# A hybrid backbone block: the short products of RWKV and of the gated DeltaNet are issued in another order and into other PSUM banks

## The chip, the cores and the metric

The kernel runs on one core of a Trainium2 chip. The metric is the device time of one execution in microseconds (us). Three executions of the kernel before are known; their median counts.

## What is computed

Four layers work on 256 context tokens and 256 latent tokens of width 1024. In each layer a norm with modulation is followed by one wide input projection, three token mixers that each scan the tokens in both directions, a gated sum, an output projection, and a mixture of 16 experts. Two of the mixers matter here, both worked out in chunks of 64 tokens:

- RWKV (8 heads of 64 channels): `S = S * w + (S a) b^T + v k^T`, `y = S r`, for each token in turn.
- GDN, the gated DeltaNet (4 heads of 128 channels), per chunk: `v_new = u - w S`, `o = qg S + A v_new`, `S = S * exp(gl) + kg^T v_new`.

The last layer needs latent tokens only, so its context scans deliver a state and no output.

## The kernel before, in words

All matrix work is fp32. A product in fp32 is two instructions in the trace (a weight load and a matmul each, twice), so counts of instructions are twice the counts of products. The dense projections (line L386) are split into a high and a low part and have one instruction for each product.

**Tokens, heads and halves.** RWKV takes two heads at a time (b = 0 to 3): head p = 0 lies in partitions 0 to 63, head p = 1 in 64 to 127. Each pair has two units (st = 0 context, st = 1 latent), each of four chunks for each direction d. A unit is `rwkv_prep` (decays and scaled keys), then `rwkv_unit`: the 64x64 systems M1, a triangular inverse, and a scan over four steps s. GDN takes one head at a time through `gdn_head`, with a scan of eight steps; its two directions are at chunks of opposite parity, so direction 0 and direction 1 are in opposite halves of the partitions.

A product whose operands lie in 64 partitions uses 64 rows of the array; one whose output has 64 partitions uses 64 columns. The trace writes rows*columns: `64*128` is half of the rows with all columns, `128*64` all rows and half of the columns, `64*64` a quarter.

**The products that the change touches** (z.mm issues one product, `mm(out, weights, moving)`):

- `rwkv_prep`, L814 and L815: for each direction two products of 64 rows by 128 columns over 256 tokens, both into one bank `pw`. In the trace: `ai<-thw,ups` and `ai<-adm,ups`. Two tanh on ScalarE (L818, L819) empty the bank.
- `rwkv_unit`, L888: for each direction and head half four products (64*128) into one bank, then one multiply on VectorE (L889). In the trace: `ai<-AR,BK`.
- `rwkv_unit`, the scan (from L921): each step makes four products of the state, `ac<-X,AR`, into bank `pu`, adds on VectorE (L931), four products with the inverse `ac<-R,Y`, two copies (L937, L938), four products `ac<-UV,BKt` (128*64) that make the next state, and the outputs: for each direction and half one product `ai<-AR,X` (64*64) and one `ai<-M,UV` (128*64) that adds to it, one behind the other, into bank `py` (L954, L955). VectorE then adds up the state (L967), copies or adds `py` to the output tile (L960, L962) and scales the state (L968); the next step's first products need that scaled state.
- `gdn_head`, the scan: each step multiplies the state of each direction with the keys and, where outputs are wanted, with the queries (`bi<-Sg,KQ`, 128*64, L1116 and L1118), makes `R` on VectorE (L1126), two products with the inverse (`bi<-R,Y`), scales on VectorE (L1133, L1135), then for each direction makes the update `bi<-v2g,Kt` (64*128, L1141) in the bank `pv` and adds it to the state on VectorE (L1146). The outputs' last products `bi<-v,Dq` go to bank `pb`.

**Banks.** RWKV's streams have two banks with the tag `ai` and one with `ac`; GDN's has two with the tag `bi`. `psm` takes the next bank of the first tag, `psc` of the second. A bank is given out again when everything that reads it is done.

**What sets the order.** The code runs through a scheduler that puts each engine's instructions in one fixed order. Every product has a due time: a stream starts at a time (`due`), and every product moves it on by its estimated length times the stream's pace (`spend`). Dense projection blocks have due times of their own and stand between the short products; so do the modulation's weights (`ada`, four products of 32 columns side by side for each row block, L305). What is ready and due first goes first. Each engine then runs its list in that order and waits on semaphores.

Of the kernel before, what the change touches and what calls it, by code (L numbers as in the profile page):

```python
# [152 lines left out]
def tile_backbone(ctx: ExitStack, tc: tile.TileContext, A, out, dbg=None, depth=DEPTH):  # L153
# [104 lines left out]
    X = {}  # L258
# [527 lines left out]
    def rwkv_prep(z, b, st, P, R, pr, noy):  # L786
# [17 lines left out]
        tk = slice(t0, t0 + 256)  # L804
# [4 lines left out]
        def c4(t):  # L809
            return t.rearrange("p (c w) -> p c w", c=4)  # L810
        for d in range(2):
            ds_ = slice(64 * d, 64 * d + 64)
            pw = z.psm()
            z.mm(pw[:, 0:256], ups[ds_, 0, :], thw[ds_, tk], start=True, stop=True)  # L814
            z.mm(pw[:, 256:512], ups[ds_, 1, :], adm[ds_, tk], start=True, stop=True)  # L815
# [52 lines left out]
    def rwkv_unit(z, b, st, vb, Y, S, noy, prep, between):  # L868
# [13 lines left out]
        for d in range(2):  # L882
            for p in range(2):
                hp = slice(64 * p, 64 * p + 64)
                ps = z.psm()
                for s in range(4):
                    c = ch(d, s)
                    z.mm(ps[:, s * 128:s * 128 + w_], BK[hp, d, c, :, :], AR[hp, d, c, 0:w_ // 64, :], start=True, stop=True)  # L888
# [33 lines left out]
        for s in range(4):  # L922
            pu = z.psc()
            rhs = Fv[:, :, s, :]
            if X is not None:
                for d in range(2):
                    for p in range(2):
                        hp = slice(64 * p, 64 * p + 64)
                        z.mm(pu[hp, d * 64:d * 64 + 64], AR[hp, d, ch(d, s), 0, :], X[hp, d, :], start=True, stop=True)
                rhs = z.mt([2, 64], "R", 2)  # L930
# [13 lines left out]
            if not noy:  # L944
                py = z.psm()
                lo_first = s < 2
                for d in range(2):
                    q = d * 4 + s
                    sl = d if lo_first else 1 - d
                    for p in range(2):  # L950
                        hp = slice(64 * p, 64 * p + 64)
                        po = py[hp, sl * 64:sl * 64 + 64]
                        if X is not None:
                            z.mm(po, X[hp, d, :], AR[hp, d, ch(d, s), 1, :], start=True, stop=False)  # L954
                        z.mm(po, UV[:, d, s, p, :], M1[:, p, d, s, 64:128], start=X is None, stop=True)  # L955
# [61 lines left out]
    def gdn_head(z, l, h, P, inputs, G, out_, oc, t):  # L1017
# [89 lines left out]
        for s in range(8):  # L1107
            wanted = s * 64 >= oc
            pv = z.psc()
            for d in range(2):  # L1110
                c = order[d][s]
                t, p = c // 2, c % 2
                hp = slice(64 * p, 64 * p + 64)
                first = Sg[d] is None
                if not first:
                    z.mm(pv[hp, 0:128], KQ[:, 0, c, :], Sg[d], start=True, stop=True)  # L1116
                    if wanted:
# [591 lines left out]
```

## Time and profile before

| what | value |
|---|---|
| median of three runs | 5302.02 us (5295.01 to 5309.08) |
| the profiled execution's own time | 5309.78 us |
| its span, first to last instruction | 5308.0 us |
| TensorE (PE) busy | 4849.0 us, 91% |
| VectorE (DVE) busy | 3129.9 us, 59% |
| ScalarE busy | 1440.6 us, 27% |
| GpSimd (POOL) busy | 1405.5 us, 26% |

Busy time of an engine is the time in which at least one of its instructions was under way. A matmul's end is modelled, so the time that a run of products really takes from the engine is read from starts: from its first start to the start of what follows it. Digits of the granted clock are tenths of full speed.

### The profile page before, as it was taken

To read this page: it belongs to the slowest core of one execution; us is meant where nothing else is said; L and a number is where in the kernel's file an instruction comes from. 1 tells how busy PE (TensorE), PEld (TensorE's weight loads), DVE (VectorE), ACT (ScalarE), POOL (GpSimd) and SP (SyncE) were. 2 spreads that over 40 slices of the span, in tenths; PEclk is the share of its full clock that TensorE was granted. 3 is DMA by queue.
4 is the path that set the end of the run, shared out by engine and by line. 5 is a ranking of instruction groups with operands and counts; after the bars stand their busy time and mean duration, and the time that the engine had idled before them with its cause. 6 is when DMAs were issued, how large, how long until landed. Compare 5 with 4: busy or idle time off the path is not lost. (4 is left out here: it accounts for less than half of the span.)

```text
span 5308.0 us, 85225 instructions
## 1 busy us (share of the span) xinstructions
PE 4849.0 (91%) x31882; PEld 3102.1 (58%) x31882; DVE 3129.9 (59%) x8787; ACT 1440.6 (27%) x2796; POOL 1405.5 (26%) x1847
## 2 busy tenths in 40 slices
PE   7999999999999999999998999999998898987798
PEld 4666666653466666666336666666633666666533
DVE  4776656633476766564347676666433677767322
ACT  3332222220233322222014222322311333322211
POOL 3332312320233222233014222222400433323400
PEclk8999999999999999999999999999999899897899
DMA  5333345579632233446983223344698222323598
GB/s 185 101 103 113 119 125 160 188 270 393 248 91 63 67 99 93 149 147 240 387 310 99 65 63 93 100 137 129 207 385 313 74 73 68 86 61 109 188 361 320
DMA packets 677006, 873.59 MB, mean 165 GB/s; under 512 B 336976, under 2 KB 359504, under 8 KB 663792
## 3 DMA queue, kind: packets, MB, share of 16 engines
q1 hardware_dynamic: 676592, 868.14, 48.5%
q8 instruction: 251, 4.11, 0.3%
q14 instruction: 163, 1.34, 0.1%
HBM read 788.47 MB, written 79.51 MB: 164 GB/s over the span
## 5 line engine op out<-in xcount | busy, mean ns | idle before, releaser
L364 POOL TENSOR_TENSOR wlo<-wraw,whi 128x512 fp32r<-128x512 f32 x696 | 942.4, 1359 | 2311.9 <-ACT whi L363 1798.6
L386 PE MATMUL df<-big,whi 128*128 128x512 f32 (+1 forms) x2944 | 982.5, 404 | 80.0 <-DVE mg L479 19.2
L386 PE MATMUL dm<-big,whi 128*128 128x512 f32 (+1 forms) x2368 | 820.0, 415 | 52.5 <-ACT cv L693 31.3
L363 ACT CAST whi<-wraw 128x512 fp32r<-128x512 f32 x696 | 426.0, 617 | 1261.5 <-PE df L386 530.7
L386 PEld LDWEIGHTS df<-big,whi 128*128 128x128 f32 x2944 | 538.4, 198 | 239.6 <-issue 51.2
L386 PE MATMUL df<-big,wlo 128*128 128x512 f32 (+1 forms) x1536 | 605.5, 394 | 22.6 <-POOL wlo L364 22.5
L386 PEld LDWEIGHTS dm<-big,whi 128*128 128x128 f32 x2368 | 447.4, 200 | 184.3 <-issue 45.0
L386 PE MATMUL dm<-big,wlo 128*128 128x512 f32 (+1 forms) x1248 | 508.0, 407 | 8.1 <-POOL wlo L364 8.1
L386 PEld LDWEIGHTS df<-big,wlo 128*128 128x128 f32 x1536 | 304.3, 198 | 86.9 <-POOL wlo L364 27.7
L1595 PE MATMUL df<-mw,big 128*64 128x512 f32 x1024 | 301.2, 610 | 0.0
L386 PEld LDWEIGHTS dm<-big,wlo 128*128 128x128 f32 x1248 | 248.3, 199 | 70.0 <-issue 16.8
L1642 DVE SCALAR_TENSOR_TENSOR big<-bi,der,big 128x256 f32<-128x256 f32 x448 | 191.9, 478 | 118.0 <-PE bi L1639 117.6
L1595 PE MATMUL dm<-mw,big 128*64 128x512 f32 x1024 | 255.5, 594 | 2.1 <-DMA mw<-in_w_dram 1.9
L984 DVE SCALAR_TENSOR_TENSOR cv<-cv,par,cv 128x189 f32<-128x189 f32 (+3 forms) x472 | 230.3, 496 | 13.0 <-ACT cv L981 10.1
L1602 POOL MEMSET mada<- 128x512 f32 x32 | 16.8, 525 | 802.7 <-PE bi L1639 350.7
L414 DVE TENSOR_TENSOR Y<-Y,sv 64x44 f32<-64x44 f32 (+6 forms) x672 | 190.2, 285 | 5.7
L413 DVE TENSOR_TENSOR sv<-Y 64x14 f32<-64x14 f32 (+6 forms) x672 | 188.7, 282 | 6.0
L1595 PEld LDWEIGHTS dm<-mw,big 128*64 128x64 f32 x1024 | 80.7, 137 | 152.4 <-issue 137.9
L697 DVE SCALAR_TENSOR_TENSOR big<-cv,muc,big 128x252 f32<-128x252 f32 (+2 forms) x280 | 140.6, 518 | 17.2 <-ACT big L694 15.5
L1633 DVE SCALAR_TENSOR_TENSOR mlof<-ac,aff,mhif 128x512 fp32r<-128x512 f32 x32 | 24.0, 750 | 212.4 <-ACT mhif L1632 212.4
L210 PE MATMUL ai<-AR,BK 64*128 64x128 f32 (+1 forms) x1024 | 144.1, 303 | 4.5 <-DVE t L775 2.8
L1629 PE MATMUL ac<-mw,mrawf 128*64 128x512 f32 x512 | 139.5, 600 | 8.6 <-ACT mrawf L1623 8.5
(511 smaller groups left out, 8334.0 us busy)
## 6 DMA issues: line engine op xcount, KB each, us to landing
mw<-in_w_dram SPq DMA_DIRECT2D x768, 512.0 KB, 10.3
wraw<-in_w_in_dram SPq DMA_DIRECT2D x536, 256.0 KB, 2.7
adaw<-in_ada_w_dram SPq DMA_DIRECT2D x96, 1024.0 KB, 5.8
gates<-gt SPq DMA_DIRECT2D x114, 256.0 KB, 2.9
wraw<-in_w_branch_dram SPq DMA_DIRECT2D x96, 256.0 KB, 3.0
TU<-zoai SPq DMA_DIRECT2D x128, 128.0 KB, 3.1
wraw<-in_w_out_dram SPq DMA_DIRECT2D x64, 256.0 KB, 5.3
t<-gates SPq DMA_DIRECT2D x61, 256.0 KB, 4.1
```

What stands on the lines that cost most here:

```text
L210: mm(o, a, b, **kw)
L363: se.copy(dst_hi, src)
L364: eng.tensor_tensor(dst_lo, src, dst_hi.bitcast(F32), ALU.subtract)
L386: mm(ps[:, c0:c1], a[:, k % 4, :], bk[:, c0:c1], start=(n == 0), stop=(n == 3 * nk - 1))
L413: ve.tensor_tensor(tv, Xb[:, j + 1:, j:j + 1].to_broadcast(sh), Xb[:, j:j + 1, 0:j].to_broadcast(sh), ALU.mult)
L414: ve.tensor_tensor(Xb[:, j + 1:, 0:j], Xb[:, j + 1:, 0:j], tv, ALU.add)
L697: ve.scalar_tensor_tensor(dst, src, muc[:, 1 + q, rb:rb + 1], dst, ALU.mult, ALU.add)
L984: ve.scalar_tensor_tensor(dst, src, cw[:, cb, t:t + 1], dst, ALU.mult, ALU.add)
L1595: mm(ps[64 * q:64 * q + 64, :], xe[k // 4][:, k % 4, e0 + q, :], wt[q][:, k2 * 512:(k2 + 1) * 512], start=(k == 0), stop=(k == 7))
L1629: mm(py[hf][64 * q:64 * q + 64, :], hT[:, kk, 64 * q:64 * q + 64], wt[q][:, hf * 512:(hf + 1) * 512], start=(kk == 0), stop=(kk == 3))
L1633: ve.scalar_tensor_tensor(yl[hf], py[hf], aff, yh[hf].bitcast(F32), ALU.mult, ALU.subtract)
L1642: ve.scalar_tensor_tensor(xT[:, db, cs_], pcb[:, cs_], der[:, 3, db, s:s + 1], xT[:, db, cs_], ALU.mult, ALU.add)
```

## The change

It reorders products and moves some to other banks; no product, copy or transfer is added or taken away.

- `rwkv_prep`: both directions' banks are taken first; the two `thw` products of the two directions are issued one behind the other, then the two `adm` products.
- `rwkv_unit`, M1: for each direction both head halves' banks are taken, and the products alternate between the halves; the two multiplies on VectorE follow behind all eight.
- The scan: bank `py` is taken at the step's start, the four `AR,X` products stand right behind the four `X,AR` products, and the four `M,UV` products stand together behind the four `UV,BKt` products. Only the first direction's product clears the bank.
- `gdn_head`: `pv` and `pb` are both taken at the step's start; the state's products go keys first for both directions, then queries; the second direction's update goes into `pb`; the two updates are issued together, and the two additions on VectorE follow.

```diff
--- before.py
+++ after.py
@@ -808,11 +808,14 @@
 
         def c4(t):
             return t.rearrange("p (c w) -> p c w", c=4)
+
+        pws = [z.psm() for d in range(2)]
+        for q, src in enumerate((thw, adm)):
+            for d in range(2):
+                ds_ = slice(64 * d, 64 * d + 64)
+                z.mm(pws[d][:, 256 * q:256 * q + 256], ups[ds_, q, :], src[ds_, tk], start=True, stop=True)
         for d in range(2):
-            ds_ = slice(64 * d, 64 * d + 64)
-            pw = z.psm()
-            z.mm(pw[:, 0:256], ups[ds_, 0, :], thw[ds_, tk], start=True, stop=True)
-            z.mm(pw[:, 256:512], ups[ds_, 1, :], adm[ds_, tk], start=True, stop=True)
+            pw = pws[d]
             sg = z.mt([256], "t1", 6)
             tha = z.mt([256], "t1", 6)
             se.activation(sg, pw[:, 0:256], AF.Tanh, scale=0.5, bias=hb[:, 0, d * 4 + b:d * 4 + b + 1])
@@ -880,12 +883,13 @@
         M1 = z.mt([2, 2, 4, 128], "M1")
         w_ = 64 if noy else 128
         for d in range(2):
-            for p in range(2):
-                hp = slice(64 * p, 64 * p + 64)
-                ps = z.psm()
-                for s in range(4):
+            pss = [z.psm() for p in range(2)]
+            for s in range(4):
+                for p in range(2):
+                    hp = slice(64 * p, 64 * p + 64)
                     c = ch(d, s)
-                    z.mm(ps[:, s * 128:s * 128 + w_], BK[hp, d, c, :, :], AR[hp, d, c, 0:w_ // 64, :], start=True, stop=True)
+                    z.mm(pss[p][:, s * 128:s * 128 + w_], BK[hp, d, c, :, :], AR[hp, d, c, 0:w_ // 64, :], start=True, stop=True)
+            for p, ps in enumerate(pss):
                 ve.tensor_tensor(M1[:, p, d, :, 0:w_], ps.rearrange("q (s w) -> q s w", s=4)[:, :, 0:w_],
                                  C[f"m1_{d}"][:, None, 0:w_].to_broadcast([128, 4, w_]), ALU.mult)
 
@@ -927,6 +931,22 @@
                     for p in range(2):
                         hp = slice(64 * p, 64 * p + 64)
                         z.mm(pu[hp, d * 64:d * 64 + 64], AR[hp, d, ch(d, s), 0, :], X[hp, d, :], start=True, stop=True)
+
+
+            lo_first = s < 2
+            po = None
+            if not noy:
+                py = z.psm()
+
+                def po(d, hp):
+                    sl = d if lo_first else 1 - d
+                    return py[hp, sl * 64:sl * 64 + 64]
+                if X is not None:
+                    for d in range(2):
+                        for p in range(2):
+                            hp = slice(64 * p, 64 * p + 64)
+                            z.mm(po(d, hp), X[hp, d, :], AR[hp, d, ch(d, s), 1, :], start=d == 0, stop=False, skip_group_check=True)
+            if X is not None:
                 rhs = z.mt([2, 64], "R", 2)
                 ve.tensor_tensor(rhs, pu[:, 0:128].rearrange("p (d w) -> p d w", d=2), Fv[:, :, s, :], ALU.add)
             for d in range(2):
@@ -942,17 +962,10 @@
                     hp = slice(64 * p, 64 * p + 64)
                     z.mm(pu[hp, 128 + d * 64:192 + d * 64], BKt[:, q, 64 * p:64 * p + 64], UV[:, d, s, p, :], start=True, stop=True)
             if not noy:
-                py = z.psm()
-                lo_first = s < 2
                 for d in range(2):
-                    q = d * 4 + s
-                    sl = d if lo_first else 1 - d
                     for p in range(2):
                         hp = slice(64 * p, 64 * p + 64)
-                        po = py[hp, sl * 64:sl * 64 + 64]
-                        if X is not None:
-                            z.mm(po, X[hp, d, :], AR[hp, d, ch(d, s), 1, :], start=True, stop=False)
-                        z.mm(po, UV[:, d, s, p, :], M1[:, p, d, s, 64:128], start=X is None, stop=True)
+                        z.mm(po(d, hp), UV[:, d, s, p, :], M1[:, p, d, s, 64:128], start=X is None and d == 0, stop=True, skip_group_check=True)
                 a, e = min(s, 3 - s), max(s, 3 - s)
                 yv = c4(Y[:, tk])[:, a::(e - a), :][:, 0:2, :]
                 pyv = py[:, 0:128].rearrange("p (d w) -> p d w", d=2)
@@ -1106,16 +1119,14 @@
         Sg = [None, None]
         for s in range(8):
             wanted = s * 64 >= oc
-            pv = z.psc()
-            for d in range(2):
-                c = order[d][s]
-                t, p = c // 2, c % 2
-                hp = slice(64 * p, 64 * p + 64)
-                first = Sg[d] is None
-                if not first:
-                    z.mm(pv[hp, 0:128], KQ[:, 0, c, :], Sg[d], start=True, stop=True)
-                    if wanted:
-                        z.mm(pv[hp, 128:256], KQ[:, 1, c, :], Sg[d], start=True, stop=True)
+            pv, pb = z.psc(), z.psm()
+            first = Sg[0] is None
+
+            for q in range(0 if first else 2 if wanted else 1):
+                for d in range(2):
+                    c = order[d][s]
+                    hp = slice(64 * (c % 2), 64 * (c % 2) + 64)
+                    z.mm(pv[hp, 128 * q:128 * q + 128], KQ[:, q, c, :], Sg[d], start=True, stop=True)
 
             R = None
             if not first:
@@ -1137,17 +1148,18 @@
                 c = order[d][s]
                 t, p = c // 2, c % 2
                 hp = slice(64 * p, 64 * p + 64)
-                pS = pv[:, 256 + 128 * d:384 + 128 * d]
-                z.mm(pS, Kt[hp, t, :], v2_[hp, :], start=True, stop=True)
+                z.mm((pv, pb)[d][:, 256:384], Kt[hp, t, :], v2_[hp, :], start=True, stop=True)
+            for d in range(2):
+                c = order[d][s]
+                t, p = c // 2, c % 2
+                pS = (pv, pb)[d][:, 256:384]
                 Sn = z.mt([128], "Sg", 4)
                 if Sg[d] is None:
                     ve.tensor_copy(Sn, pS)
                 else:
                     ve.scalar_tensor_tensor(Sn, Sg[d], eL[:, p, t, d, h:h + 1], pS, ALU.mult, ALU.add)
-                first = Sg[d] is None
                 Sg[d] = Sn
             if wanted:
-                pb = z.psm()
                 for d in range(2):
                     c = order[d][s]
                     t, p = c // 2, c % 2
```

## Rows read from the trace of the kernel before

**Rows 1.** The page, parts 1 and 2: TensorE's busy time and granted clock in 40 slices.
```profile
PE 4849.0 (91%) x31882; PEld 3102.1 (58%) x31882; DVE 3129.9 (59%) x8787; ACT 1440.6 (27%) x2796; POOL 1405.5 (26%) x1847
...
PEclk8999999999999999999999999999999899897899
```

**Rows 2.** Busy time by stretch, all engines: the mixers of layers 1 and 3.
```profile
1498.00:2310.00 812.00, 762.82 (x5947) 530.34 (x5948) 553.47 (x1690) 234.67 (x477) 221.11 (x341) 0.97 0.32 96
...
4189.00:4935.00 746.00, 653.67 (x5608) 506.67 (x5608) 544.75 (x1651) 225.78 (x487) 250.15 (x364) 0.90 0.29 80
```

**Rows 3.** Groups by line on PE: xinstructions | busy us, mean ns | idle before, releasers.
```profile
L210 PE MATMUL ai<-AR,BK 64*128 64x128 f32 (+1 forms) x1024 | 144.1, 303 | 4.5 <-DVE t L775 2.8 <-DVE M L889 1.6
L210 PE MATMUL bi<-Sg,KQ 128*64 128x128 f32 x848 | 139.9, 287 | 0.8 <-DVE Sg L1146 0.5 <-ACT ob L1160 0.3
L210 PE MATMUL ai<-M,UV 128*64 128x64 f32 x896 | 138.0, 241 | 1.0 <-DVE UV L937 0.9
L210 PE MATMUL ai<-AR,X 64*64 64x64 f32 x800 | 126.2, 238 | 1.4 <-DVE Y L440 1.2
L210 PE MATMUL bi<-v2g,Kt 64*128 64x128 f32 x512 | 123.5, 321 | 11.6 <-DVE v L1135 6.9 <-DVE Sg L1146 3.0 <-DVE v2g L1133 1.2
...
L210 PE MATMUL ai<-thw,ups 64*128 64x256 f32 x128 | 44.9, 432 | 5.2 <-DVE Y L414 2.2 <-ACT t L819 2.0 <-DVE sv L413 0.9
...
L210 PE MATMUL ai<-adm,ups 64*128 64x256 f32 x128 | 38.8, 386 | 0.0
```

**Rows 4.** Timeline of PE in an RWKV scan: start us, us, engine line op.
```profile
2025.30 0.45 PE L210 MATMUL ac<-UV,BKt 128*64 128x64 f32 x8
2025.58 0.40 PE L210 MATMUL ai<-M,UV 128*64 128x64 f32 x6
2025.91 0.50 PE L386 MATMUL df<-big,wlo 128*128 128x512 f32 x1
...
2029.82 0.32 PE L210 MATMUL ai<-AR,X 64*64 64x64 f32 x2
...
2031.36 0.73 PE L386 MATMUL df<-big,whi 128*128 128x512 f32 x2
...
2032.25 0.45 PE L210 MATMUL ac<-X,AR 64*64 64x64 f32 x8
2032.53 0.28 PE L210 MATMUL ai<-AR,X 64*64 64x64 f32 x2
```

**Rows 5.** Timeline of VectorE in the same step of the scan.
```profile
2031.46 0.29 DVE L960 COPY big<-ai 128x128 f32<-128x128 f32 x1 [1.23 <-PE ai L210]
2031.67 0.28 DVE L968 TENSOR_TENSOR X<-X,scl 128x128 f32<-128x128 f32 x1
```

**Rows 6.** Two stretches of 0.44 us within one run of AR,BK, by tile BK.
```profile
133.02:133.46 0.44, 0.44 (x4) 0.44 (x5) 0.00 (x0) 0.00 (x0) 1.00 0.00 0
133.50:133.94 0.44, 0.44 (x10) 0.44 (x9) 0.00 (x0) 0.00 (x0) 1.00 0.00 0
```

**Rows 7.** Timeline of PE in a GDN scan.
```profile
2060.32 0.48 PE L210 MATMUL bi<-v2g,Kt 64*128 64x128 f32 x2
2060.73 0.43 PE L210 MATMUL bi<-v,Dq 64*64 64x128 f32 x4
...
2061.96 0.65 PE L210 MATMUL bi<-Sg,KQ 128*64 128x128 f32 x4
2062.54 1.12 PE L210 MATMUL ai<-t,cst 128*128 128x512 f32 x2
...
2070.61 0.66 PE L210 MATMUL bi<-Sg,KQ 128*64 128x128 f32 x8
2071.21 0.72 PE L386 MATMUL df<-big,whi 128*128 128x512 f32 x2
```

**Rows 8.** Groups by line and form on VectorE and ScalarE: what empties RWKV's banks.
```profile
L889 DVE TENSOR_TENSOR M<-ai,cst 128x512 f32<-128x512 f32 x112 | 76.7, 688 | 83.4 <-PE ai L210 82.8
...
L818 ACT ACTIVATE t<-ai,hb 128x256 f32<-128x256 f32 x64 | 30.0, 469 | 9.2 <-PE ai L210 8.9
```

## Prediction

> **What bounds the kernel now.** I read the page first. TensorE (PE) is busy 91% of the span, and its granted clock is full speed in all but a few slices [rows 1]. Busy time by stretch then places it: in the three mixers' stretch of layer 1 PE is busy 762.82 of 812 us, VectorE 553.47, at a granted clock of 0.97; in layer 3, whose fillers are half as wide, 653.67 of 746 at 0.90 [rows 2]. So PE sets the pace in the mixers of layers 0 to 2, where all the touched products lie, and a little less in layer 3. The groups by line give the size of what is touched: M1's `AR,BK` 144.1 us, the GDN state products `Sg,KQ` 139.9, the outputs `M,UV` 138.0 and `AR,X` 126.2, the GDN updates `v2g,Kt` 123.5, the prep's two groups 44.9 and 38.8 [rows 3]. That is 755 us of busy time, and hardly any of it is waiting.
>
> Busy time alone doesn't say what a reorder can save; the timeline does. Within one run of `AR,BK` the array goes through a stretch of 0.44 us with 4 instructions while one half of the rows is used, and through an equal stretch with 10 when the second half's products, in the other bank, have come up behind the first's [rows 6]. So two row halves run at once when they write different banks, and the engine starts the second half a little ahead of its turn. Eight instructions of `Sg,KQ` that stand together, both directions, take from 2070.61 to 2071.21, 0.60 us; four of one direction alone take 0.58 [rows 7]. So column halves pair as well. The cost of the old order is that partners seldom stand side by side.
>
> **The change part by part.** Every saving below is PE time, read from starts.
>
> *The scan's outputs.* Three alternating pairs of `AR,X` and `M,UV` take from 2029.82 to 2031.36, 1.54 us, 0.26 for each product [rows 4]. The trace has both shapes in good company: four `X,AR` products take 2032.25 to 2032.53, 0.28 us, and four `UV,BKt` products 2025.30 to 2025.58, also 0.28, which is 0.07 for each product; there, in a unit's first step, where no `AR,X` exists, the `M,UV` products already follow directly [rows 4]. After the change three products of each kind join such runs: 6 x 0.07 = 0.42 us. The saving is 1.54 - 0.42 = 1.1 us a step. There are 800 / 8 = 100 such steps [rows 3], so 112 us. Bounds: 80, if the outputs' runs stand alone and pay for another change of tile shape (about 0.3 us a step), and 130, with the step's first `AR,X` counted too. I take 112, since the code issues them directly behind their like.
>
> [...] The four `X,AR` products use opposite quarters of the array, write one bank, and still need only 0.07 us each [rows 4], and `AR,X` has that very shape. [...]
>
> *M1.* One half streams an instruction in 0.44 / 4 = 0.11 us [rows 6]. For one direction eight products, 16 instructions, paired throughout need 8 x 0.11 plus about 0.2 at the ends, 1.1 us; 64 directions (32 units) make 70 us against 144.1 now [rows 3], a saving of 74 at most. At least it is nothing: the old order already overlaps where two sets meet, and the second direction now waits for the two banks one after the other, as the two multiplies (688 ns each [rows 8]) release them, so its first half may run ahead alone. I take 45, three fifths.
>
> *Prep.* 44.9 + 38.8 = 83.7 us [rows 3]; perfect pairs save 42, none 0. Both products are ready together, but both banks must be free and another stream's product may slip between. I take 25.
>
> *GDN's state products.* A step with outputs pays 2 x 0.58 now and 0.60 when all four stand together [rows 7]: 0.56 saved in 100 of the steps (848 instructions are 84 steps with eight in the first three layers, 16 in the last, and 12 with four [rows 3]), 56 at most. The second direction's state is ready one addition after the first's, so the first may be issued alone as before: at least 0. I take half, 28.
>
> *GDN's updates.* Each takes 2060.32 to 2060.73, 0.41 us [rows 7], and 512 / 4 = 128 steps have two [rows 3]. Their inputs come from one scaling, and they no longer wait for the other's addition in a shared bank. Paired, the two cost about one: 52 saved. Unpaired in one run they still save one change of shape, about 0.2, 26 us. I take 45.
>
> *Banks and waits.* `pb` is now taken at a step's start; it was emptied a scaling, two products and an addition before its first writer, so this costs nothing, and without that cover the wait would be a copy of 0.3 us. `py` is held from the first product of a step instead of the last ones; the next prep is done before the scan starts, so nobody wants it. No DMA moves, and no instruction on the queues of SP and POOL.
>
> The sum is 112 + 45 + 25 + 28 + 45 = 255 us of PE time. How much of it comes off the end? In layers 0 to 2 PE is 94% busy and dense blocks fill what is freed, so I count 0.85; in layer 3 (88% busy, lower clock) 0.6. At a fifth of the sum in layer 3: 204 x 0.85 + 51 x 0.6 = 204 us. The RWKV chain doesn't stand against it: the output copy at 2031.46 waits 1.23 us for the outputs' products, and the scaling of the state at 2031.67 stands queued behind it on VectorE, though its own input had long been ready [rows 5]. The next step's first products wait for that scaling, so those 1.1 us a step are on the chain too. Late next are the dependent steps themselves: VectorE's short operations and the inverse's round trip.
>
> The profiled execution took 5309.78 us, 7.8 above the median of the runs. 5309.8 - 204 = 5106, and beside the median **5098 us**.
>
> **The rivals.** *The chain sets the mixers' length.* For it: each unit's M1, inverse and scan depend on one another, and PE's 6% idle time in layer 1 stays small only as long as fillers last. Against it: PE is busy nearly throughout [rows 2]. Then only what lies on the chain counts, the outputs' 112 us: about 5190.
>
> *Row halves don't pair.* Then M1 and prep give nothing and the updates 26. The three `AR,X` products of a step, six instructions at the 0.11 us of an unpaired half [rows 6], cost 0.66 instead of 0.21, so the outputs lose 45 of their 112: 67 + 28 + 26 = 121, of which 0.8 is 97, so 5205. [...] [Rows 6] speak against the rest, but show 128 columns in one place only.
>
> *The pairs are torn apart.* The scheduler puts dense blocks or the other stream between partners and the saved shape changes come back elsewhere: within 0.3% of 5302. Against it: `X,AR` stands in eights.
>
> *Slower: both of RWKV's banks are closed at once.* M1's and prep's products now fill both banks together, so nothing of RWKV can use one while VectorE or ScalarE empties the other. Price: for each unit two multiplies of 0.69 us that used to run beside products, and four tanh of 0.47 [rows 8], 1.4 + 1.9 = 3.3 us, times 32 units 105 us: 5407. It decides only if RWKV's chain sets the length and the saved 1.1 us a step are lost to another wait.
>
> **How the numbers follow.** A difference under 0.3% (16 us) can't be told from none. Chances: the forecast 0.62, the chain 0.22, no pairing of rows 0.06, torn pairs 0.04, slower 0.06. Faster is the sum of the first three, 0.90. The lower end takes all upper bounds, 130 + 74 + 42 + 56 + 52 = 354, at 0.85 to 0.9: about 310 us, 4990. The upper end takes the chain and the unpaired rows with some room, 5240; the other two cases, 0.10, and some of the tails are left out.
>
> **What would show it.** Right: the groups `AR,X` and `M,UV` fall from 126 and 138 us to about half or less, with runs of eight behind `X,AR` and `UV,BKt`; `v2g,Kt` stands in fours; VectorE's copy of `py` no longer waits over a microsecond before the scaling; PE's busy time in the mixers falls by some 200 us at much the same share. Chain: PE's share in the mixers drops to about 85% and the stretches shrink by under 30 us each. Unpaired rows: `v2g,Kt` in fours of about 0.6 us. Closed banks: long waits of `AR,BK` or `thw,ups` for VectorE and ScalarE, and units further apart. The forecast is wrong if the short groups shrink and the mixers don't.

## The result, and the profile after

The changed kernel takes 5150.62 us (median of four runs, 5146.26 to 5153.63) beside 5305.55 for the kernel before on the same chip (four runs, 5295.01 to 5318.0). The ratio is 0.9706, 95% interval 0.9683 to 0.973: 155 us or 2.9% faster. The forecast was 5098, its range 4990 to 5240. The profiled execution took 5153.63 us with a span of 5151.7, 156.3 us less than before.

The page of the kernel after, parts 1 and 2, TensorE's busy time and granted clock, beside [rows 1]:

```profile
PE 4671.7 (91%) x31882; PEld 2965.9 (58%) x31882; DVE 3135.1 (61%) x8787; ACT 1437.8 (28%) x2796; POOL 1401.7 (27%) x1847
...
PEclk8999999999999999999999999999999899987899
```

The number of instructions is the same and TensorE's busy time is 177 us lower, at the same share of the span. So the gain fits TensorE time that is no longer needed, 0.88 of which came off the end; the experiments below take the parts apart. Busy time by stretch of the kernel after (span of the stretch, then each engine's busy time and count, granted clock, DMA), the mixers of layers 1 and 3, beside [rows 2]:

```profile
1458.00:2217.00 759.00, 711.25 (x5956) 489.95 (x5957) 556.06 (x1691) 234.39 (x479) 220.43 (x342) 0.96 0.34 103
4050.00:4777.00 727.00, 625.29 (x5606) 486.07 (x5605) 542.08 (x1648) 225.65 (x487) 250.19 (x364) 0.89 0.30 82
```

Layer 1's stretch is 53 us shorter for 51.5 us less of TensorE; layer 3's 19 for 28. TensorE's share is 94% as before and 86% (88 before): freed time in layer 1 turns into length in full, in layer 3 by two thirds.

The groups by line on PE (instructions, then busy us and mean ns of one, then idle before them and releasers), beside [rows 3]:

```profile
L210 PE MATMUL ai<-AR,BK 64*128 64x128 f32 (+1 forms) x1024 | 133.4, 308 | 10.4 <-DVE M L893 6.1 <-DVE t L775 1.8 <-POOL BK L867 1.5
...
L210 PE MATMUL bi<-Sg,KQ 128*64 128x128 f32 x848 | 87.7, 287 | 4.4 <-ACT ob L1172 2.2 <-DVE Sg L1160 1.9
L210 PE MATMUL bi<-v2g,Kt 64*128 64x128 f32 x512 | 87.4, 324 | 9.1 <-DVE v2g L1144 8.8 <-DVE v L1146 0.3
...
L210 PE MATMUL ai<-M,UV 128*64 128x64 f32 x896 | 82.6, 229 | 1.9 <-DVE UV L957 1.5
...
L210 PE MATMUL ai<-thw,ups 64*128 64x256 f32 x128 | 45.0, 433 | 3.4 <-DVE sv L413 3.4
...
L210 PE MATMUL ai<-AR,X 64*64 64x64 f32 x800 | 44.4, 221 | 1.6 <-DVE Y L440 1.6
...
L210 PE MATMUL ai<-adm,ups 64*128 64x256 f32 x128 | 39.5, 389 | 0.0
```

Four groups fell far; `AR,BK` fell by 11, the prep's two not at all. Busy time counts pairs that run at once only once, and ends are modelled, so I also summed, for every instruction of a group, the time from its start to the next instruction's start without idle time. These sums, in us, are what the rest of the text calls TensorE time:

| group | before | after | saved | forecast |
|---|---|---|---|---|
| scan: `AR,X`, `M,UV` with `X,AR`, `UV,BKt` beside them | 276.1 | 168.6 | 107.5 | 112 |
| M1: `AR,BK` | 132.2 | 123.2 | 9.0 | 45 |
| prep: `thw`, `adm` | 69.0 | 70.1 | -1.1 | 25 |
| GDN state products: `Sg,KQ` | 122.3 | 75.1 | 47.2 | 28 |
| GDN updates: `v2g,Kt` | 104.3 | 74.2 | 30.1 | 45 |
| dense projections, L386 | 2131 | 2156 | -25 | 0 |
| all of TensorE | 4849 | 4672 | 177 | 255 |

**The scan.** PE's timeline of the kernel after (start, us, operation, tiles, shape, count), one step, beside [rows 4]:

```profile
1952.09 0.33 PE L210 MATMUL ai<-M,UV 128*64 128x64 f32 x2
...
1952.78 0.45 PE L210 MATMUL ac<-UV,BKt 128*64 128x64 f32 x8
1953.06 0.40 PE L210 MATMUL ai<-M,UV 128*64 128x64 f32 x6
1953.40 0.50 PE L386 MATMUL df<-big,whi 128*128 128x512 f32 x1
...
1954.75 0.45 PE L210 MATMUL ac<-X,AR 64*64 64x64 f32 x8
1955.03 0.40 PE L210 MATMUL ai<-AR,X 64*64 64x64 f32 x8
```

From 1953.06 to 1953.40 three outputs pass in 0.34 us behind their like; before, one product of the alternating run cost 0.26. The eight `AR,X` instructions do the same behind `X,AR`. VectorE's timeline of that step, beside [rows 5]; a bracket would show a wait:

```profile
1953.46 0.29 DVE L980 TENSOR_TENSOR X<-ac,X 128x128 f32<-128x128 f32 x1
...
1953.78 0.28 DVE L973 COPY big<-ai 128x128 f32<-128x128 f32 x1
...
1954.09 0.28 DVE L981 TENSOR_TENSOR X<-X,scl 128x128 f32<-128x128 f32 x1
```

The output copy (L973) no longer waits 1.23 us in front of the scaling (L981).

**GDN.** PE's timeline of the kernel after, beside [rows 7]:

```profile
1979.00 0.49 PE L210 MATMUL bi<-v2g,Kt 64*128 64x128 f32 x4
1979.42 0.50 PE L386 MATMUL df<-big,whi 128*128 128x512 f32 x1
...
1986.67 0.66 PE L210 MATMUL bi<-Sg,KQ 128*64 128x128 f32 x8
1987.26 0.50 PE L386 MATMUL df<-big,whi 128*128 128x512 f32 x1
...
1990.40 0.49 PE L210 MATMUL bi<-v2g,Kt 64*128 64x128 f32 x2 [0.45 <-DVE v2g L1144]
1990.81 0.50 PE L386 MATMUL dm<-big,whi 128*128 128x512 f32 x1
1991.24 0.48 PE L210 MATMUL bi<-v2g,Kt 64*128 64x128 f32 x2
```

Eight `Sg,KQ` take 0.59 us, and 74 such eights stand in the trace, 5 before. Four `v2g,Kt` together take 0.42 us, two alone 0.41; in 80 of the 128 steps the two directions stand together.

**M1 and prep.** PE's timeline of the kernel after, an M1 and a prep:

```profile
133.87 1.16 PE L210 MATMUL ai<-AR,BK 64*128 64x128 f32 x16
...
135.87 1.31 PE L210 MATMUL ai<-AR,BK 64*128 64x128 f32 x10
...
138.23 0.71 PE L210 MATMUL ai<-AR,BK 64*128 64x128 f32 x6
...
1981.82 0.70 PE L210 MATMUL ai<-thw,ups 64*128 64x256 f32 x2
1982.35 0.59 PE L210 MATMUL ai<-adm,ups 64*128 64x256 f32 x2
1982.87 0.43 PE L210 MATMUL bi<-R,Y 64*64 64x128 f32 x4
1983.24 0.70 PE L210 MATMUL ai<-thw,ups 64*128 64x256 f32 x2
1983.78 0.59 PE L210 MATMUL ai<-adm,ups 64*128 64x256 f32 x2
```

Here M1's first direction runs as one sixteen, paired, in about 1.1 us (14 runs in the trace have sixteen instructions); the second is torn in ten and six, 2.4 us apart. The prep still issues one direction's two products and then the other's. The fixed order that the scheduler wrote says the same of every unit: in prep it is `thw`, `adm`, `thw`, `adm` in all 32, as before; M1's halves alternate fully in 22 of 32 units for direction 0 and in 6 for direction 1.

### The profile page after: what moved, and what is told of

Same layout as the page of the kernel before. It is cut to its first block, busy times and chain, and to the rows that moved or that the text cites. A ratio compares the mean times of both kernels' runs of the same rounds, so it can differ in the third digit from the quotient of the medians.

```text
span 5151.7 us, 85291 instructions
## 1 busy us (share of the span) xinstructions
PE 4671.7 (91%) x31882; PEld 2965.9 (58%) x31882; DVE 3135.1 (61%) x8787; ACT 1437.8 (28%) x2796; POOL 1401.7 (27%) x1847
## 5 line engine op out<-in xcount | busy, mean ns | idle before, releaser
L386 PE MATMUL df<-big,whi 128*128 128x512 f32 (+1 forms) x2944 | 1001.9, 408 | 87.6 <-ACT gt L546 19.7
L386 PE MATMUL dm<-big,whi 128*128 128x512 f32 (+1 forms) x2368 | 821.2, 415 | 44.6 <-ACT cv L693 31.7
L386 PEld LDWEIGHTS df<-big,whi 128*128 128x128 f32 x2944 | 545.8, 200 | 253.9 <-issue 46.9
L386 PE MATMUL df<-big,wlo 128*128 128x512 f32 (+1 forms) x1536 | 612.0, 398 | 16.6 <-POOL wlo L364 16.6
L386 PEld LDWEIGHTS dm<-big,whi 128*128 128x128 f32 x2368 | 443.0, 199 | 174.6 <-issue 40.5
L386 PE MATMUL dm<-big,wlo 128*128 128x512 f32 (+1 forms) x1248 | 505.6, 405 | 18.3 <-POOL wlo L364 18.3
L386 PEld LDWEIGHTS df<-big,wlo 128*128 128x128 f32 x1536 | 306.3, 199 | 83.8 <-POOL wlo L364 20.9
L386 PEld LDWEIGHTS dm<-big,wlo 128*128 128x128 f32 x1248 | 248.1, 199 | 81.2 <-POOL wlo L364 22.7
L414 DVE TENSOR_TENSOR Y<-Y,sv 64x14 f32<-64x14 f32 (+6 forms) x672 | 193.6, 290 | 5.6
L210 PE MATMUL ai<-AR,BK 64*128 64x128 f32 (+1 forms) x1024 | 133.4, 308 | 10.4 <-DVE M L893 6.1
```

Of the source, the lines that this page charges most:

```text
L210: mm(o, a, b, **kw)
L386: mm(ps[:, c0:c1], a[:, k % 4, :], bk[:, c0:c1], start=(n == 0), stop=(n == 3 * nk - 1))
L414: ve.tensor_tensor(Xb[:, j + 1:, 0:j], Xb[:, j + 1:, 0:j], tv, ALU.add)
```

## The experiments

My theory after the result: the mixers pay for TensorE time, the saving is the scan's and GDN's, and the forecast fell short of 255 because the pairs of M1 and prep were torn by their banks. The main rivals: RWKV's dependent chain is what was shortened; and saved TensorE time is worth less than it seems. Each measured ratio is to the kernel before, run on the same chip beside it.

### The parts alone

The scan's part of the change alone, on the kernel before:

```diff
+            if not noy:
+                py = z.psm()
...
+                            z.mm(po(d, hp), X[hp, d, :], AR[hp, d, ch(d, s), 1, :], start=d == 0, stop=False, skip_group_check=True)
...
-                            z.mm(po, X[hp, d, :], AR[hp, d, ch(d, s), 1, :], start=True, stop=False)
```

> Only the RWKV scan's outputs are moved. Theory (PE time is the bound, and about 0.88 of what a part frees on PE comes off the end: the whole change freed 177 us by starts and gave 156): AR,X, M,UV and the runs they join free about 112 us, so about 5206 us against 5305. Rival (RWKV's chain is the bound): this part is the only one on the chain, so it gives nearly all of the change's 155 us, about 5155.

Measured: 5224.24 us against 5304.21, ratio 0.9848 (0.9832 to 0.9865), 80 us. The four groups fell from 276.1 to 167.8, all of TensorE by 83. That is nearer to the theory than to the rival, but a step of the scan got shorter too: from one `UV,BKt` run to the next of its unit it takes 5.49 us, 6.37 before (medians of 96). This run alone doesn't separate TensorE's time from the chain.

GDN's part alone:

```diff
+            pv, pb = z.psc(), z.psm()
...
+            for q in range(0 if first else 2 if wanted else 1):
+                for d in range(2):
...
+                z.mm((pv, pb)[d][:, 256:384], Kt[hp, t, :], v2_[hp, :], start=True, stop=True)
```

> Only GDN's two edits. Theory (PE time): Sg,KQ and v2g,Kt free about 75 us, so about 5239 us. Rival (RWKV's chain): GDN's stream is not on it, so within 10 us of 5305.

Measured: 5263.18 us, ratio 0.9923 (0.9908 to 0.9938), 41 us. `Sg,KQ` fell to 75.1 and `v2g,Kt` to 78.9; all of TensorE by 51, short of the 75 that the theory had. RWKV's stream, whose dependent steps this edit leaves alone, got shorter by as much: from its first prep to its last `UV,BKt` of a layer it takes 3222 us in the sum of the four layers, 3265 before, and TensorE's idle time stayed (436 and 438). So the gain reached RWKV through TensorE.

Prep and M1 alone:

```diff
+        pws = [z.psm() for d in range(2)]
...
+            pss = [z.psm() for p in range(2)]
+            for s in range(4):
+                for p in range(2):
```

> Only the order of prep's and M1's products. Theory (the pairs don't form, since the two banks come free one after the other and whichever product has its bank goes alone): thw,ups and adm,ups stay at about 75 us by starts, AR,BK falls by about 9; the time is 5290 to 5305, within what can be told. Rival (the order works, and the other parts hid it in the whole change): AR,BK and the prep fall by 40 us or more and the time to about 5265.

Measured: 5311.61 us, ratio 1.0015 (0.9998 to 1.0032): nothing. `AR,BK` fell to 118.2, prep stayed at 69.1, and the dense products grew from 2131 to 2154, so all of TensorE rose by 13.

The change without prep and M1 (both other parts together):

```diff
-        pws = [z.psm() for d in range(2)]
...
-            pss = [z.psm() for p in range(2)]
```

> The change without prep's and M1's part. Theory (these two parts did nothing): 5150 to 5165 us, within 15 us of the whole change. Rival (they gave their forecast 70 us of PE time): about 5210.

Measured: 5172.81 us, ratio 0.9747 (0.9726 to 0.9768), 131 us, above the 5150 to 5165 of the theory. The two parts alone gave 80 and 41, 121 in sum. The whole change is 22 us better (the intervals of the two ratios still touch), with `AR,BK` at 123.2 instead of 141.6 and `v2g,Kt` at 74.2 instead of 84.9. So prep and M1 are worth nothing alone and a little beside the rest; the rise of the dense products (2152 here, 2156 in the whole change) is there with or without them.

### GDN: the order of the state products, or the banks of the updates?

Only the order of the state products, on the kernel before:

```diff
+            for q in range(0 if first else 2 if wanted else 1):
+                for d in range(2):
...
-                    z.mm(pv[hp, 0:128], KQ[:, 0, c, :], Sg[d], start=True, stop=True)
```

> The kernel before with only the order of GDN's state products changed: keys of both directions, then queries of both; the updates stay in one bank, one behind the other's addition. Theory (the pairs come from the two states being ready together, not from the order in the code): Sg,KQ stays above 110 us by starts, the time is 5290 to 5325. Rival (the order makes the pairs): Sg,KQ falls to about 75 us and the time to about 5265.

Measured: 5316.37 us against 5305.89, ratio 1.0021 (1.0004 to 1.0037). The order alone gives no time. `Sg,KQ` did fall to 105.3, below the 110 of the theory: in 91 steps the first direction's product with the keys goes alone and the other three follow together. But all of TensorE rose by 13, with dense products that cost 25 us more. VectorE's timeline of this kernel, the two additions of a step:

```profile
2067.81 0.35 DVE L1143 SCALAR_TENSOR_TENSOR Sg<-Sg,eg,bi 128x128 f32<-128x128 f32 x1 [1.10 <-PE ai L210]
2068.98 0.35 DVE L1143 SCALAR_TENSOR_TENSOR Sg<-Sg,eg,bi 128x128 f32<-128x128 f32 x1 [0.82 <-PE bi L210]
```

The second direction's state is ready 1.17 us after the first's (1.46 in the median of all steps), since its update shares a bank with the first addition; in most steps the first direction's product has been issued by then.

Only the updates in two banks, with the additions behind both, in the old order of the state products:

```diff
-                pS = pv[:, 256 + 128 * d:384 + 128 * d]
-                z.mm(pS, Kt[hp, t, :], v2_[hp, :], start=True, stop=True)
+                z.mm((pv, pb)[d][:, 256:384], Kt[hp, t, :], v2_[hp, :], start=True, stop=True)
```

> The kernel before with only GDN's updates in two banks, both issued ahead of the two additions; the state products keep the old order, two of one direction, then two of the other. Theory (both states come ready together, and the engine starts the second direction's products ahead of its turn where they stand directly behind): Sg,KQ falls to about 75 to 85 us and v2g,Kt to about 80 by starts, as in gdn_only, so 5255 to 5275 us. Rival (the order is needed as well): Sg,KQ stays near 120 us and the time near 5290.

Measured: 5263.71 us, ratio 0.9925 (0.9905 to 0.9944): all of what GDN's part gives. `Sg,KQ` fell to 80.0 here too, `v2g,Kt` to 84.2. VectorE's two additions of a step and then PE's timeline of this kernel:

```profile
2067.30 0.61 DVE L1147 SCALAR_TENSOR_TENSOR Sg<-Sg,eg,bi 128x128 f32<-128x128 f32 x2
```

```profile
2069.62 0.67 PE L210 MATMUL bi<-Sg,KQ 128*64 128x128 f32 x8
2070.22 0.50 PE L386 MATMUL dm<-big,whi 128*128 128x512 f32 x1
```

The two additions now follow each other 0.26 us apart in the median (1.44 in the kernel before), so both states are ready together and both directions' four stand together; and though two products of one direction stand ahead of the other's, the eight take the same 0.6 us. The saving on `Sg,KQ`, which the forecast gave to the order, is made for the most part by the banks of the updates: they alone save 42 us, the order alone 17, both together 47.

### Is it RWKV's chain?

The copy of Y moved behind the scaling of the state, on the kernel before:

```diff
-                if lo_first:
-                    ve.tensor_copy(yv, pyv)
...
             if X is not None:
...
+            if not noy:
...
+                if lo_first:
+                    ve.tensor_copy(yv, pyv)
```

> The kernel before, with one VectorE step moved: in each scan step the copy of the outputs stands behind the state's scaling instead of ahead of it, so that the state no longer waits for the outputs' products. PE's products and their order by the code are untouched. Theory (PE time is the bound): PE has as much to do as before, so 5285 to 5310 us. Rival (RWKV's chain is the bound): about 1 us a step comes off the chain, 100 steps, so about 5205.

Measured: 5328.11 us against 5304.21, ratio 1.0048 (1.0029 to 1.0068). That is above both forecasts, and the record doesn't show why. A step got shorter (5.97 us, 6.37 before), but by less than half of the expected 1 us, and RWKV's stream as a whole didn't (3267 and 3265 us). Taking the waiting copy out of the way gives no gain.

The outputs, held in their old order, issued a step later, behind the next step's `R,Y` products:

```diff
+            if late:
+                late()
...
-            if not noy:
+            def outputs(s=s, X=X):
...
+            late = None if noy else outputs
```

> The kernel before with one edit: each scan step's output products (the four AR,X and four M,UV, in the old order and bank, with the copy of Y) are issued one step later, behind the R,Y products of the next step, so that TensorE's work stays as it was and only its place changes: the outputs no longer stand between the state products of one step and the X products of the next. Theory (the outputs' TensorE time counted nearly in full because it stood on RWKV's dependent path): at least half of the 80 us that the scan part alone gave come from the move alone, so 5265 us or less. Rival (only TensorE's time counts, wherever it stands): the work is the same and the time stays within 5290 to 5320 us.

Measured: 5342.48 us against 5312.8, ratio 1.0055 (1.0036 to 1.0074). PE's timeline of this kernel:

```profile
1585.27 0.45 PE L210 MATMUL ac<-UV,BKt 128*64 128x64 f32 x8 [0.36 <-DVE UV L941]
...
1587.51 0.45 PE L210 MATMUL ac<-X,AR 64*64 64x64 f32 x8
...
1589.27 0.45 PE L210 MATMUL ac<-R,Y 64*64 64x64 f32 x8
1589.55 0.28 PE L210 MATMUL ai<-AR,X 64*64 64x64 f32 x2
1589.76 0.33 PE L210 MATMUL ai<-M,UV 128*64 128x64 f32 x2
...
1592.91 0.28 PE L210 MATMUL ac<-UV,BKt 128*64 128x64 f32 x2
```

From `UV,BKt` to the next `X,AR` the median over the scan's steps is 1.94 us, 3.13 before: there the outputs are out of the way. But they now stand between `R,Y` and `UV,BKt`, where it is 2.72 us instead of 1.86, and the whole round, from one `UV,BKt` run to the next of its unit, is as long as before: 6.34 us, 6.37 before (5.23 after the change). The four groups' TensorE time rose to 309.0, all of it by 48, and the time by 30, above both forecasts; TensorE also ran 563 us at the lower level of its clock, 498 before (the two levels are 0.50 and 1.00: in the kernel after, for one, 0.50 from 34 to 54 us and 1.00 from 56 to 80). So this run doesn't tell what the place of the outputs is worth: the edit takes them out of one part of the dependent round and puts them in another, where they cost more.

### Can the torn pairs be held together?

In the whole change, prep's and M1's products are held in alternating order, beginning with the bank that is free last:

```diff
+    def mms(self, products):
+        for i, (o, a, b) in enumerate(products):
+            ins = self.mm(o, a, b, start=True, stop=True)
+            if i:
+                tc.keep_in_program_order(ins)
```

> The whole change, with prep's and M1's products held in the alternating order: the one whose bank comes free last is first, and each later one is kept behind the one before it, so that a pair waits until both banks are free. Theory (the bank that comes free first tore the pairs): prep's two groups fall from 74 to about 40 us by starts, AR,BK from 132 to about 80, some 85 us of PE time, and the time falls by 40 to 75 us, to 5075 to 5110. Rival (row halves with 256 columns don't pair, or the wait for both banks lengthens RWKV's chain by as much): the groups don't fall, or the time stays at 5150 or above.

Measured: 5154.17 us against 5304.21, ratio 0.9723 (0.9703 to 0.9743): no better than the change, as the rival had it. The page of this kernel, part 1 and the granted clock, and its PE timeline of an M1's second direction and a prep:

```profile
PE 4657.3 (90%) x31882; PEld 2942.9 (57%) x31882; DVE 3110.0 (60%) x8787; ACT 1441.5 (28%) x2796; POOL 1401.6 (27%) x1847
...
PEclk8999999999999999999999999999999899887799
```

```profile
136.74 0.46 PE L210 MATMUL ai<-AR,BK 64*128 64x128 f32 x2
...
142.42 0.70 PE L210 MATMUL ai<-thw,ups 64*128 64x256 f32 x2
...
149.44 0.48 PE L210 MATMUL ai<-thw,ups 64*128 64x256 f32 x1
149.45 0.48 PE L210 MATMUL ai<-adm,ups 64*128 64x256 f32 x1
149.76 0.38 PE L210 MATMUL ai<-thw,ups 64*128 64x256 f32 x1
149.77 0.80 PE L210 MATMUL ai<-adm,ups 64*128 64x256 f32 x3
```

The fixed order now alternates in all 32 units, and where `thw` and `adm` stand in opposite row halves they start 0.01 us apart. TensorE time fell in both groups, M1's to 107.6 and prep's to 57.6, but that is 28 us together where the theory had some 85. The order is held, the pairs aren't: the first product stands alone, with other products behind it, in 49 of the 64 directions of M1 (11 in the change) and in 31 of the 32 preps. What full pairs would give is not shown.

All of TensorE's time fell by only 14 against the change, and its idle time rose from 460 to 485 us, 7 of these 25 just before M1's and prep's products; what made the rest isn't shown. The trace is of this kernel's slowest execution, 5164.73 us. The mean granted clock is 0.947 (0.950 in the change): 550 us at the lower level, 519 in the change. The time is the same.

GDN's state products and updates held in the same way as well:

```diff
+            z.mms([((pv, pb)[d][:, 256:384], Kt[half(d), order[d][s] // 2, :], v2_[half(d), :]) for d in (1, 0)])
```

> As paired_rwkv, with GDN's state products and updates held in pairs as well, the second direction first. Theory (pairs save wherever they form): v2g,Kt falls from 74 to about 57 us, Sg,KQ from 77 to about 68, so another 10 to 25 us off paired_rwkv. Rival (holding the first direction back until the second's state is ready lengthens GDN's chain, or fillers part them still): no faster than paired_rwkv.

Measured: 5172.0 us, ratio 0.9762 (0.9738 to 0.9787): slower than the change. `Sg,KQ` fell to 68.4, but the granted clock is 0.943, 587 us lie at the lower level, idle time is 476 us, and all of TensorE's time is 4667, 5 us below the change and 10 above the kernel with M1's and prep's order held.

Prep's second bank taken from the other tag, which frees at another time:

```diff
-        pws = [z.psm() for d in range(2)]
+        pws = [z.psm(), z.psc()]
```

> The whole change, with the second of prep's two banks taken from the scan's single bank, which is free during the prep. Theory (a pair needs both banks at the same moment; another bank only changes which product goes alone first): no more than a quarter of the preps pair, thw,ups and adm,ups stay above 65 us by starts, the time is 5140 to 5165. Rival (there is simply one bank too few): the pairs form, the groups fall to about 40 us and the time to about 5120.

Measured: 5159.54 us, ratio 0.9729 (0.9711 to 0.9748). Prep took 73.7; its order begins with both `thw` in only 5 of 32 units. In the other 27 the second direction, whose bank is now the scan's, has both its products ahead of the first's, as if whichever bank was free first went first.

### What is a microsecond of TensorE worth?

Each of prep's products issued twice, the same value into the same place:

```diff
+                for _ in range(2):
+                    z.mm(pws[d][:, 256 * q:256 * q + 256], ups[ds_, q, :], src[ds_, tk], start=True, stop=True)
```

> The whole change, with each of prep's products issued twice into the same place (the second overwrites the first): 128 products, about 70 us more of PE time by starts, off RWKV's serial chain. Theory (PE time is the bound, and it counts at 0.8 to 0.9): 55 to 65 us more than the change, 5205 to 5220. Rival (chains of dependent steps set the mixers' length, PE's work fits beside them): within 20 us of the change, at most 5170.

Measured: 5166.76 us against 5305.89, ratio 0.9743 (0.9721 to 0.9766), 16 us above the change: the rival's forecast came true, not the theory's. The groups by line on PE of this kernel:

```profile
L210 PE MATMUL ai<-thw,ups 64*128 64x256 f32 x256 | 80.8, 431 | 0.2
...
L210 PE MATMUL ai<-adm,ups 64*128 64x256 f32 x256 | 75.2, 418 | 0.0
```

Prep's TensorE time rose by 62.5 and all of TensorE's by 59, while its idle time fell by 33. Between a quarter and a half of the rise became time (16 us between medians, 27 in the span of the profiled execution). Saved time in the scan and in GDN came off at 0.8 to nearly 1 (80 of 83, 41 of 51); extra time in prep is swallowed by idle time for the larger part. So in this kernel what a microsecond of TensorE is worth depends on where it stands. At this rate the 14 us that the held order saved would give 4 to 6, too little to be told from none.

## Why the prediction was right, and where its terms were off

The forecast case held: for the scan and GDN a saving of TensorE's time came off the end (80 of 83 and 41 of 51 us in the parts alone), and pairs that stand together made it (eight `Sg,KQ` in 0.59 us, four of one direction alone in 0.58). The median lies in the range, 53 us above the forecast. The sum of 255 us measured 177; the share that came off the end was 0.88 instead of 0.8. So the miss lies in the sum, and the low share hid a part of it: 204 us forecast, 156 measured.

- **The scan's outputs: 112, measured 107.5.** Right in size and in kind: the shapes that stood in good company in [rows 4] give about the same pitch when the outputs join them: four `AR,X` products take 0.33 us (1955.03 to 1955.36), the four `X,AR` ahead of them 0.28. All eight `AR,X` instructions write one bank, from opposite quarters of the array, and need no more than that. One `M,UV` product still goes alone in many steps, 0.26 us, because the first half's copy is ready before the second's (1952.09 above), and the step's first `AR,X`, which the 112 left out, joins its run instead. No run shows the price of a change of tile shape (0.3 us a step in the lower bound here, 0.2 in that of GDN's updates) by itself: those were estimates, and what the runs show is 0.26 us for a product among others [rows 4] and 0.08 in the run of four `AR,X`.
- **M1: 45, measured 9** (18 against the kernel with the other two parts). Two steps failed. One is in the prediction's own words: the second direction "waits for the two banks one after the other, as the two multiplies release them, so its first half may run ahead alone". I saw it and still took three fifths. It is the rule, not the exception: only 6 of 32 units alternate there. The other is the price. The bound of 74 takes 144.1 us of busy time for the old order, where by starts it is 132.2, and 1.1 us for a paired direction. A direction that alternates takes 1.6 us in the mean (1.59 for 22 first ones, 1.68 for 6 second ones), as other products still come between; with all 64 held in that order M1 takes 107.6 us, not 70.
- **Prep: 25, measured nothing.** "Both products are ready together, but both banks must be free" names what happened: not one of 32 units paired, and in the run with another second bank one direction went wholly ahead of the other in 27 of them. The bound was off here as well: 42 is half of 83.7 us of busy time, and by starts the two groups take 69.0. Holding the order brought 57.6 us although most first products still stood alone; partners that do stand side by side start 0.01 us apart there (149.44 and 149.45), so these two do run together where they meet.
- **GDN's state products: 28, measured 47, and GDN's updates: 45, measured 30.** Their sum, 73, measured 77, so the kind was right and the shares were not. "The second direction's state is ready one addition after the first's, so the first may be issued alone" was false once the updates had two banks: the additions follow each other, and eights became the rule. The cause of most of that saving is the updates' banks, not the order I credited.
- **Dense products: I had nothing for them, measured +25.** They stand in 1384 unbroken runs after the change, 1289 before, and every variant with a part of the change shows them 13 to 30 us dearer. A dense product alone between short ones takes 0.43 us from start to start (1990.81 to 1991.24), against 0.23 inside a run, so 95 more runs can account for some 19 us by an estimate from these two. The clock adds to it: TensorE ran 519 us at the lower level, 498 before. Two runs set the two apart: with the bank of prep's second direction changed, 1372 runs and 493 us at the lower level, dense products cost 21 us more than before; with the outputs a step later, 1278 runs and 563 us, 10 us more. So both count, and in the change the runs count for more.
- **What comes off the end.** Layer 1 gave all and layer 3 two thirds; I had 0.85 and 0.6. The reason that I added, that the output copy's 1.23 us wait [rows 5] lies on RWKV's chain, found no support: taking the copy out of the way gained nothing, and the run with the outputs moved left the dependent round as long as before.
- **The rivals.** *The chain sets the length* (5190) fails as it was put: GDN's part, off RWKV's chain, gave 41 us alone. But extra TensorE time in prep was swallowed by idle time for the larger part, so dependent steps do set a part of the length, and for the scan's 80 us, where the steps got shorter too, the runs don't separate the two. *Row halves don't pair* fails: sixteen `AR,BK` that alternate take 1.09 us (133.87 above), where sixteen of the kernel before took 1.64 (223.28 to 224.92). *Torn pairs* was given 0.04 as an all or nothing case; it came true for two of the five terms. *Both banks closed at once* shows as idle time before `AR,BK`, 10.4 instead of 4.5 us, not the 105 us of its price.

## What to carry to other kernels

Before counting on a pair, look at when each partner's bank and input come free: the scheduler here, which places what is ready first, brought GDN's updates, whose banks are both taken at the step's start, together in 80 of 128 steps, and tore M1's second direction (alternating fully in 6 of 32 units) and prep (in none), whose banks, as I read it, open one after the other, though the code had them in pairs. Where inputs come apart because two results share a bank, give them two banks first: here the two additions came 0.26 us apart instead of 1.44, and `Sg,KQ` fell from 122.3 to 80.0 us with the order of the code left as it was. And a forced order is not yet a pair: here other products still came between, and the time stayed the same (5154.17 us beside 5150.62).

## What the hardware showed

- Products on different halves of the columns start ahead of their turn, as far as starts tell. With the updates in two banks and the old order, both products of one direction stand before both of the other; the eight instructions still start in twos, 13 ns apart, and take 0.594 us in the median of 77 such runs, 0.587 in the new order. In one of them six of the eight matmuls are under way within the first 0.29 us. Span of the stretch, then PE, weight loads and VectorE, granted clock, DMA, of the instructions with tile `Sg` alone:

```profile
2054.57:2054.86 0.29, 0.29 (x6) 0.29 (x8) 0.00 (x0) 1.00 0.00 0
2054.86:2055.16 0.30, 0.30 (x8) 0.13 (x4) 0.00 (x0) 1.00 0.00 0
```

  The trace doesn't name the halves: that they alternate is read from the starts, since the eight take hardly longer than the 0.58 us that four of one direction take alone [rows 7]. How far ahead this reaches isn't shown; eight `AR,BK` of one half followed by eight of the other overlap in part only [rows 6].
- The clock took part of the saved TensorE time back, by an estimate. The change spent 519 us at the lower of the two granted levels (0.50; the other is 1.00), the kernel before 498, where the prediction read full speed in all but a few slices [rows 1]; the kernel with M1's and prep's order held 550, the one with GDN's held as well 587. Inside dense runs a product of 512 columns takes 0.43 us there from start to start and 0.23 at the upper level (medians of 266 and 5269 in the change), so nearly half of the time at the lower level is lost if all of it is like this: 14 and 31 us more than in the change, beside the 28 and 35 us that M1, prep and `Sg,KQ` had saved. The last layer's mixers, at 0.89 in the change, are one place where it shows. Busy time by that stretch (columns as above) of the kernel with M1's and prep's order held:

```profile
4050.00:4777.00 727.00, 618.20 (x5495) 476.04 (x5495) 535.16 (x1635) 226.09 (x487) 253.30 (x364) 0.88 0.30 82
```

And of the kernel with GDN's held as well, where it is 0.87:

```profile
4050.00:4777.00 727.00, 619.31 (x5548) 482.58 (x5546) 544.74 (x1652) 230.59 (x499) 247.04 (x366) 0.87 0.30 83
```

Only the clock compares here: 111 and 58 fewer TensorE instructions than in the change (5606) fall into the window, so the busy times are not for the same work.
